# Joined decay products, joined rope products and a tile of their own for the experts' scaled outputs in a fused two-block transformer

## The chip, the cores and the metric

The program runs on one core of one Trainium2 chip. The metric is the device time of one execution in microseconds, from three executions: a median of 2303.01, with 2300.93 and 2308.81 as the ends. One further execution was profiled.

## The reference, cut to what matters

One sequence of 512 rows (16 meta rows are added for the first block) with 1024 features goes through three layers. All arithmetic is float32.

```python
# first block: differential attention + convolution, then 16 experts that each choose 66 rows
h = h + expert_choice_ffn(rms_norm(h, ffn_norm_g), w_router, w_gate, w_up, w_down)
# second block, layer 1 (mlstm): four heads; weights of the past decay by sums of log f
d = b[..., :, None] - b[..., None, :] + ib[..., None, :]
p = einsum("bhtd,bhsd->bhts", q, k) * exp(d - m_t)
# second block, layer 2 (mla): eight heads; a score has a part of 128 features and a rope part of 64
sc = einsum("bqhd,bkhd->bhqk", q, k) * QK_HEAD ** -0.5      # QK_HEAD = 128 + 64
```

Each expert computes `(silu(x @ w_gate) * (x @ w_up)) @ w_down`, scales the result by the row's gate and adds it to the rows that it chose.

## The kernel before, in words

A float32 product is made of TensorE products in a float32 format of fewer bits: an operand is split into a high part (ScalarE copy, `K.split`, L191 or L164 for weights) and a low part, the remainder (VectorE, L192 or L165), and high-high, low-high and high-low are added in PSUM (`TRIPLES`). Nearly all products go through `K.mm` (L198), so rows of the profile are told apart by their tiles. Instructions are written in the program's order by generators that are interleaved by weights, and a scheduler then sets the order on each engine; only TensorE's order in the experts is pinned (`K.pin`). On ScalarE and VectorE the order is kept once it is set: an instruction that waits holds those behind it.

**Experts** (about 370 to 1480 us). Weights come as 384 loads of 1 MB, queued on SP by `w_dma` (L138) into a ring of 17 buffers (`K.ring`). For each load two ScalarE copies (`wh`, L164) and two VectorE remainders (`wl`, L165) are made into four buffers each, so these run a few products ahead of TensorE. For each expert and each half f of its hidden features, TensorE makes G (gate), then U (up); ScalarE takes silu of G into tile `sa` (L1029), VectorE multiplies by U (L1033), TensorE transposes the product. After both halves TensorE makes Y (down). `scatter` (L992, L993) scales Y into `ys`, which is again a tile `sa`, of which there is one buffer, and GpSimd issues an indirect DMA that adds it to `acc_d` in DRAM. The next expert's silu of its first half writes the same buffer, so it waits until that DMA has read it. PSUM holds one buffer each for G, U, Y and T; G of the second half may start only when silu has read G of the first. The tiles `K.xs` (four of 128x1024) hold the residual rows before the experts; they are written out to `acc_d` ahead of the experts and loaded again from it at expert 14.

**mLSTM layer** (about 1480 to 1920 us). Gate pre-activations of the four heads are made as rows (`ig`, `fg`, 4x512), and a chain on VectorE gives `bm` and, per chunk S and later chunk T, the sums `tot`. Tile `RR` (128x512, zeroed on GpSimd) holds chunk S's rows on partitions 32S to 32S+3, and is split into `R2` (high, low). In `gen_attn`, for each head and S, the decay exponents reach all partitions by two products of four rows each (`sel[d, h]` with high and low, `S<-R,cr` in the trace, 512 - 128S columns) and a causal mask product (`S<-cr`, 128 columns). Then follow the products of q and k (`S<-q,k`) and projections of other heads (`P`).

**MLA layer** (about 1920 to 2306 us). Per pair of heads, `gen_T` transposes q and k through the PSUM tile `T` (two buffers): `qT`, `kT` for the 128 features, `qpT`, `kpT` for the rope features, where head 0 of the pair lies on partitions 0 to 63 and head 1 on 64 to 127. `gen_attn` makes, for each head and query tile t, scores of 128(t+1) columns: three products of 128 rows (`S<-kT,qT`), three of 64 rows (`S<-kpT,qpT`) and a mask (`S<-maskr`, 128 columns). `softmax_T` takes the maximum, the exponential into one of three `e` buffers, scales and transposes it (L1206, `T<-ident,e`), `K.split` fills `pT`, and after four tiles the products with v follow. Beside it run projections (`P`) of the next pairs. `rope_rows` (L1770 to L1772) makes the rope of a q pair from one GpSimd and two VectorE operations for each half, with a temporary tile `rb2` of its own.

## Time and profile before

| | us |
|---|---|
| median of three runs (lowest, highest) | 2303.01 (2300.93, 2308.81) |
| the profiled execution | 2307.86 |
| its span, first to last instruction | 2306.1 |
| TensorE busy | 2200.1 (95%) |
| VectorE busy | 1774.5 (77%) |
| ScalarE busy | 1469.8 (64%) |
| GpSimd busy | 235.5 (10%) |

The time of the profiled execution is 1.8 us longer than its span and 4.85 us (0.2%) above the median. Busy time of TensorE is the union of its matmuls, which are pipelined: the distance between two starts, not the length of one, tells what a matmul costs in a stream.

### The profile page before, as it was taken

To read this page: it belongs to the slowest core of one execution; us is meant where nothing else is said; L and a number is where in the kernel's file an instruction comes from. 1 tells how busy PE (TensorE), PEld (TensorE's weight loads), DVE (VectorE), ACT (ScalarE), POOL (GpSimd) and SP (SyncE) were. 2 spreads that over 40 slices of the span, in tenths; PEclk is the share of its full clock that TensorE was granted. 3 is DMA by queue.
4 is the path that set the end of the run, shared out by engine and by line. 5 is a ranking of instruction groups with operands and counts; after the bars stand their busy time and mean duration, and the time that the engine had idled before them with its cause. 6 is when DMAs were issued, how large, how long until landed. Compare 5 with 4: busy or idle time off the path is not lost.

```text
span 2306.1 us, 33188 instructions
## 1 busy us (share of the span) xinstructions
PE 2200.1 (95%) x12311; PEld 1647.0 (71%) x12311; DVE 1774.5 (77%) x2615; ACT 1469.8 (64%) x2193; POOL 235.5 (10%) x248
## 2 busy tenths in 40 slices
PE   7899988999999999999999999899999999899999
PEld 6899875655555555555555555688888899777779
DVE  5966577988888888888898899866665746676762
ACT  4765346777777777777777788754454624555551
POOL 2111261000000000000000011410000000010000
PEclk9999998999999999999999999999999999999999
DMA  5312778999999999999999799342322233211122
GB/s 176 88 56 67 259 276 300 378 376 359 379 369 371 371 367 365 370 372 372 374 365 364 294 376 386 130 156 76 103 90 73 83 120 114 66 49 60 51 92 74
DMA packets 204416, 528.56 MB, mean 229 GB/s; under 512 B 13362, under 2 KB 94896, under 8 KB 204254
## 3 DMA queue, kind: packets, MB, share of 16 engines
q1 hardware_dynamic: 196157, 507.64, 60.7%
q0 software_dynamic: 5488, 13.93, 2.3%
q10 hardware_dynamic: 2608, 4.87, 0.6%
q8 instruction: 97, 1.59, 0.3%
q14 instruction: 66, 0.53, 0.1%
HBM read 506.41 MB, written 17.82 MB: 227 GB/s over the span
## 4 chain that ended last, share of the span: by engine, by line
PE 79%; ACT 3%; DVE 2%; issue 1%; DMA 0%; POOL 0%; SPq 0%; ACTq 0%; DVEq 0%; POOLq 0%
PE P L198 24%; PE G L198 16%; PE Y L198 15%; PE U L198 14%; PE S L198 4%; PE O L198 3%; PE T L203 1%; DVE wl L165 1%; ACT wh L164 1%; ACT sa L1029 1%; PE T L1880 0%; PE T L1206 0%; PE T L1173 0%; PE T L1104 0%; DMA xg<-hn_d,idx 0%
## 5 line engine op out<-in xcount | busy, mean ns | idle before, releaser
L165 DVE TENSOR_TENSOR wl<-raw,wh 128x1024 fp32r<-128x1024 f32 (+1 forms) x586 | 710.0, 1224 | 150.7 <-ACT wh L164 139.5
L164 ACT ACTIVATE wh<-raw 128x1024 fp32r<-128x1024 f32 (+1 forms) x604 | 634.6, 1056 | 274.7 <-PE P L198 64.5
L198 PE MATMUL G<-wh,xgT 128*66 128x512 f32 x1024 | 280.7, 396 | 21.5 <-ACT sa L1029 20.7
L198 PE MATMUL Y<-wh,hT 128*66 128x512 f32 x1024 | 278.4, 393 | 0.0
L198 PE MATMUL U<-wh,xgT 128*66 128x512 f32 x1024 | 277.9, 393 | 0.0
L165 DVE TENSOR_TENSOR wl<-h,wh 128x1024 fp32r<-128x1024 f32 x196 | 239.5, 1237 | 26.6 <-ACT wh L164 22.8
L198 PE MATMUL P<-hT,wh 128*128 128x512 f32 x768 | 247.7, 395 | 0.0
L164 ACT ACTIVATE wh<-h 128x1024 fp32r<-128x1024 f32 x200 | 210.7, 1060 | 57.1 <-PE G L198 22.5
L198 PEld LDWEIGHTS G<-wh,xgT 128*66 128x66 f32 x1024 | 138.2, 137 | 120.1 <-ACT sa L1029 27.0
L198 PEld LDWEIGHTS U<-wh,xgT 128*66 128x66 f32 x1024 | 139.9, 137 | 97.0
L198 PEld LDWEIGHTS Y<-wh,hT 128*66 128x66 f32 x1024 | 137.4, 137 | 90.6
L198 PEld LDWEIGHTS P<-hT,wh 128*128 128x128 f32 x768 | 143.4, 188 | 29.3
L198 PE MATMUL U<-wl,xgT 128*66 128x512 f32 x512 | 159.9, 394 | 0.8 <-DVE wl L165 0.8
L198 PE MATMUL G<-wl,xgT 128*66 128x512 f32 x512 | 160.2, 394 | 0.0
L198 PE MATMUL Y<-wl,hT 128*66 128x512 f32 x512 | 159.8, 393 | 0.0
L198 PE MATMUL P<-wh,hT 128*128 128x256 f32 (+2 forms) x712 | 148.4, 291 | 5.5 <-ACT hT L191 3.2
L198 PE MATMUL P<-hT,wl 128*128 128x512 f32 x384 | 151.3, 394 | 0.0
L165 DVE TENSOR_TENSOR wl<-mx,wh 128x1024 fp32r<-128x1024 f32 x96 | 116.8, 1228 | 13.8 <-ACT wh L164 12.2
L198 PE MATMUL P<-h,wh 128*128 128x264 f32 x640 | 122.5, 286 | 1.8 <-ACT qraw L427 1.0
L198 PEld LDWEIGHTS P<-wh,hT 128*128 128x128 f32 x712 | 117.3, 191 | 7.6 <-ACT hT L191 3.9
L164 ACT ACTIVATE wh<-mx 128x1024 fp32r<-128x1024 f32 x96 | 101.3, 1061 | 27.3 <-PE Y L198 9.6
L198 PE MATMUL P<-wl,hT 128*128 128x256 f32 (+2 forms) x408 | 117.0, 289 | 0.0
(648 smaller groups left out, 3918.7 us busy)
## 6 DMA issues: line engine op xcount, KB each, us to landing
raw<-w_gate SPq DMA_DIRECT2D x82, 1024.0 KB, 7.1
raw<-w_down SPq DMA_DIRECT2D x80, 1024.0 KB, 9.1
raw<-w_up SPq DMA_DIRECT2D x76, 1024.0 KB, 7.2
h<-w_up SPq DMA_DIRECT2D x35, 1024.0 KB, 6.7
h<-w_down SPq DMA_DIRECT2D x32, 1024.0 KB, 8.9
h<-w_gate SPq DMA_DIRECT2D x31, 1024.0 KB, 6.9
raw<-a_w_in SPq DMA_DIRECT2D x24, 1024.0 KB, 5.5
mx<-w_up SPq DMA_DIRECT2D x17, 1024.0 KB, 7.2
```

Of the source, the lines that this page charges most:

```text
L164: self.nc.scalar.activation(hv, v[:, r], AF.Copy)
L165: lo.tensor_tensor(lv, v[:, r], hv.bitcast(F32), op=OP.subtract)
L198: self.last_mm = self.nc.tensor.matmul(out, l, r, start=st, stop=sp)
L203: i = self.nc.tensor.transpose(out, src, ident)
L1029: silu = nc.scalar.activation(hh, g[:CAP], AF.Silu)
```

## The change

It has three parts.

1. Experts: `ys` is no longer a tile `sa` but the first 66 rows of `K.xs[e % 2]`, two buffers that lie idle between the writing of `acc_d` and its loading.
2. mLSTM layer: the gate rows are made twice (weights and biases doubled, 8 rows instead of 4). `RR` becomes two tiles of 8 rows (from the `hn` buffers), whose columns hold the chunks one behind the other (512 + 384 + 256 + 128 = 1280). `R2` becomes one tile of 128 x 1280, zeroed on GpSimd; rows 0 to 3 hold the high parts and rows 4 to 7 the low parts: ScalarE rounds, and VectorE makes `rounded * low + r` with `low` 0 or -1. `sel` has a one in rows h and 4+h. A decay tile is then one product of 128 rows instead of two of 4.
3. MLA layer: `qpT[i]` holds head i's high parts on its own 64 partitions and its low parts on the other 64; `kpT[i][0]` holds head i's high parts on both halves and `kpT[i][1]` its low parts on both. The rope scores are then two products of 128 rows instead of three of 64 (low-low comes in besides). For this, `qpT` takes 2 ScalarE and 2 VectorE operations of 64 rows instead of 1 and 1 of 128, and `kpT` 4 and 4 instead of 1 and 1, for each of four pairs, and two tiles of 128x512 more. Room for these is made by `pT` with 10 blocks instead of 13, which for t = 2 and 3 is filled by two splits instead of one (16 ScalarE and 16 VectorE operations more in all), and by the rope's temporary, which now takes one of the three `e` buffers.

```diff
--- before.py
+++ after.py
@@ -41,9 +41,10 @@
     slot = np.broadcast_to(np.arange(1, CAP + 1, dtype=np.float32), (128, CAP))
     sel = np.zeros((128, 4), np.float32)
     for h in range(4):
-        sel[h::32, h] = 1.0
+        sel[[h, 4 + h], h] = 1.0
     ntri = np.where(p[None, :] > p[:, None], -1e30, 0.0).astype(np.float32)
-    out["c_mask"] = np.concatenate([sel, ntri], 1)
+    low = np.where((p >= 4) & (p < 8), -1.0, 0.0).astype(np.float32)[:, None]
+    out["c_mask"] = np.concatenate([sel, ntri, low], 1)
     bm = np.where((p[:, None] < 64) & (p[None, :] >= 64), -1e30, 0.0)
     out["c_bmisc"] = np.concatenate([np.broadcast_to(inv, (128, 32)), bm], 1).astype(np.float32)
     out["c_iota"] = np.arange(128, dtype=np.float32)[None, :]
@@ -988,10 +989,10 @@
 
     def scatter(y, e):
 
-        ys = K.t(p, [CAP, 2, 512], F32, "sa")
-        nc.scalar.activation(ys, y[:CAP], AF.Copy, scale=K.gate[:, e:e + 1])
+        ys = K.xs[e % 2][:CAP]
+        nc.scalar.activation(ys.rearrange("p (a b) -> p a b", a=2), y[:CAP], AF.Copy, scale=K.gate[:, e:e + 1])
         nc.gpsimd.indirect_dma_start(out=K.acc_d, out_offset=bass.IndirectOffsetOnAxis(ap=K.idx[:, e:e + 1], axis=0),
-                                     in_=ys.rearrange("p a b -> p (a b)"), in_offset=None, compute_op=OP.add)
+                                     in_=ys, in_offset=None, compute_op=OP.add)
         gather(K, e + 2)
         if e == K.ne - 2:
             for t in range(4):
...
@@ -1306,11 +1308,12 @@
 def a_pre2(K):
     nc, p, ident = K.nc, K.pools["apre"], K.ident
     w8, cs2 = K.src
-    wif = K.t(p, [128, 8, 36], F32, "wif")
+    wif = K.t(p, [128, 8, 40], F32, "wif")
     nc.gpsimd.memset(wif, 0.0)
-    nc.gpsimd.tensor_copy(wif[:, :, 0:4], w8[:, :, 0:4])
-    nc.gpsimd.tensor_copy(wif[:, :, 32:36], w8[:, :, 4:8])
-    K.wifs = [K.t(p, [128, 8, 36], F32R, f"wif{i}") for i in range(2)]
+    for i in (0, 4):
+        nc.gpsimd.tensor_copy(wif[:, :, i:i + 4], w8[:, :, 0:4])
+        nc.gpsimd.tensor_copy(wif[:, :, 32 + i:36 + i], w8[:, :, 4:8])
+    K.wifs = [K.t(p, [128, 8, 40], F32R, f"wif{i}") for i in range(2)]
     K.split(K.wifs[0], K.wifs[1], wif)
     K.cr = K.t(p, [128, 6, 128], F32R, "cr")
     nc.gpsimd.tensor_copy(K.cr[:, 0:4], cs2[:, 0:4, None].to_broadcast([128, 4, 128]))
@@ -1409,14 +1412,17 @@
     cr = K.t(p1, [128, 6, 128], F32R, "cr")
     nc.gpsimd.tensor_copy(cr, K.cr)
     sel = cr[:, 0:4]
+    offs = [0, 512, 896, 1152]
+    R2 = K.t(p1, [128, 1280], F32R, "R2")
+    nc.gpsimd.memset(R2.bitcast(F32), 0.0)
 
 
     o = K.t(ps, [128, 512], F32, "P", 3)
-    K.acc(o[:36], [(K.wifs[a][:, k], hT[b][:, k]) for k in range(8) for a, b in TRIPLES])
-    row = lambda name: K.t(p, [4, 512], F32, name)
+    K.acc(o[:40], [(K.wifs[a][:, k], hT[b][:, k]) for k in range(8) for a, b in TRIPLES])
+    row = lambda name: K.t(p, [8, 512], F32, name)
     ig, f, t1, t2, lf = row("ig"), row("fg"), row("t1"), row("t2"), row("lf")
-    nc.vector.tensor_scalar(ig, o[0:4], K.gb[:, 0:1], None, op0=OP.add)
-    nc.vector.tensor_scalar(f, o[32:36], K.gb[:, 1:2], None, op0=OP.add)
+    nc.vector.tensor_scalar(ig, o[0:8], K.gb[:, 0:1], None, op0=OP.add)
+    nc.vector.tensor_scalar(f, o[32:40], K.gb[:, 1:2], None, op0=OP.add)
     nc.vector.tensor_scalar_mul(t1, f, -1.0)
     nc.vector.tensor_tensor(t1, t1, f, op=OP.min)
     nc.scalar.activation(t1, t1, AF.Exp)
@@ -1432,7 +1438,7 @@
     bm = row("t1")
     nc.vector.tensor_sub(bm, b, m)
     nc.vector.tensor_sub(ig, ig, b)
-    tot = K.t(p, [4, 4, 4], F32, "tot")
+    tot = K.t(p, [8, 4, 4], F32, "tot")
     for S in range(4):
         for T in range(S + 1, 4):
             e = b[:, 128 * T - 1:128 * T]
@@ -1440,21 +1446,23 @@
                 nc.vector.tensor_copy(tot[:, S, T:T + 1], e)
             else:
                 nc.vector.tensor_add(tot[:, S, T:T + 1], tot[:, S, T - 1:T], e)
-    RR = K.t(p, [128, 512], F32, "RR")
-    nc.gpsimd.memset(RR, 0.0)
+
+    RR = [K.t(p, [128, D], F32, "hn", 2)[:8] for _ in range(2)]
     for S in range(4):
-        d = slice(32 * S, 32 * S + 4)
-        nc.vector.tensor_copy(RR[d, 128 * S:128 * S + 128], bm[:, 128 * S:128 * S + 128])
+        r, of = RR[S // 2], offs[S] - offs[S // 2 * 2]
+        nc.vector.tensor_copy(r[:, of:of + 128], bm[:, 128 * S:128 * S + 128])
         for T in range(S + 1, 4):
-            ts = slice(128 * T, 128 * T + 128)
-            nc.vector.tensor_scalar(RR[d, ts], bm[:, ts], tot[:, S, T:T + 1], None, op0=OP.add)
-    R2 = [K.t(p1, [128, 512], F32R, f"R{i}") for i in range(2)]
-    K.split(R2[0], R2[1], RR)
+            at = of + 128 * (T - S)
+            nc.vector.tensor_scalar(r[:, at:at + 128], bm[:, 128 * T:128 * T + 128], tot[:, S, T:T + 1], None, op0=OP.add)
+    for r, (a_, b_) in zip(RR, ((0, 896), (896, 1280))):
+        rt = R2[:8, a_:b_]
+        nc.scalar.activation(rt, r[:, :b_ - a_], AF.Copy)
+        nc.vector.scalar_tensor_tensor(rt, rt.bitcast(F32), K.src[1][:8, 132:133], r[:, :b_ - a_], op0=OP.mult, op1=OP.add)
     o = K.t(ps, [128, 512], F32, "T", 2)
     for t in range(4):
         ts = slice(128 * t, 128 * t + 128)
-        nc.tensor.transpose(o[:, 8 * t:8 * t + 4], ig[:, ts], ident[:4, :4])
-        nc.tensor.transpose(o[:, 8 * t + 4:8 * t + 8], m[:, ts], ident[:4, :4])
+        nc.tensor.transpose(o[:, 8 * t:8 * t + 4], ig[:4, ts], ident[:4, :4])
+        nc.tensor.transpose(o[:, 8 * t + 4:8 * t + 8], m[:4, ts], ident[:4, :4])
     cb = K.t(p1, [128, 4, 8], F32, "cb")
     nc.vector.tensor_copy(cb, o[:, :32].rearrange("p (t x) -> p t x", x=8))
     em = K.t(p1, [128, 4, 4], F32, "em")
@@ -1465,7 +1473,6 @@
     p = pa_.enter_context(tc.tile_pool(name="a2", bufs=1, reuse_waits="tile"))
     K.p_pq = tc.tile_pool(name="aq", bufs=1, side="right", reuse_waits="tile")
     pq = K.p_pq.__enter__()
-    offs = [0, 512, 896, 1152]
     qkv = {("v", 0): v0}
 
     def gen_v(h):
@@ -1515,10 +1522,8 @@
         for S in range(4):
             n = 512 - 128 * S
             ss = slice(128 * S, 128 * S + 128)
-            d = slice(32 * S, 32 * S + 4)
             bc = K.t(ps, [128, 512], F32, "S", 2)
-            K.mm(bc[:, :n], sel[d, h], R2[0][d, 128 * S:], True, False)
-            K.mm(bc[:, :n], sel[d, h], R2[1][d, 128 * S:], False, False)
+            K.mm(bc[:, :n], sel[:, h], R2[:, offs[S]:offs[S] + n], True, False)
             K.mm(bc[:, :128], cr[:, 4], cr[:, 5], False, True)
             wt = K.t(p, [128, 512], F32, "e", 3)
             nc.scalar.activation(wt[:, :n], bc[:, :n], AF.Exp, bias=cb[:, S, h:h + 1])
@@ -1766,7 +1771,8 @@
         x1, x2 = src[:, :, :, 0:32], src[:, :, :, 32:64]
         d1, d2 = dst[:, :, :, 0:32], dst[:, :, :, 32:64]
         for d, a, b, op in ((d1, cos, sin, OP.subtract), (d2, sin, cos, OP.add)):
-            tb = K.t(pool, sh, F32, f"rb{heads}")
+            tb = K.t(pool, sh, F32, "rb1") if heads == 1 else \
+                K.t(pool, [128, 512], F32, "e", 3)[:, :256].rearrange("p (t h d) -> p t h d", t=4, h=2)
             nc.gpsimd.tensor_tensor(d, x1, a, op=OP.mult)
             nc.vector.tensor_mul(tb, x2, b)
             nc.vector.tensor_tensor(d, d, tb, op=op)
@@ -1870,6 +1876,9 @@
         qkv["kv", pr] = ks, kp, v
         yield 0
 
+    BASE = (0, 3, 5, 6)
+    HALVES = [(slice(0, 64), slice(64, 128)), (slice(64, 128), slice(0, 64))]
+
     def gen_T(pr):
         qs, qp, rq = qkv["q", pr]
         ks, kp, v = qkv["kv", pr]
@@ -1878,8 +1887,25 @@
             o = K.t(ps, [128, 4, 128], F32, "T", 2)
             for t in range(4):
                 nc.tensor.transpose(o[:, t], src(t), ident)
+            o = o.rearrange("p t s -> p (t s)")
+            if name == "qpT":
+
+                d = [K.t(pq, [128, 512], F32R, f"{name}{i}") for i in range(2)]
+                for i, (r, x) in enumerate(HALVES):
+                    nc.scalar.activation(d[i][r], o[r], AF.Copy)
+                    nc.vector.tensor_sub(d[i][x], o[r], d[i][r].bitcast(F32))
+                return d
+            if name == "kpT":
+
+                d = [[K.t(pq, [128, 512], F32R, f"{name}{i}{b}") for b in range(2)] for i in range(2)]
+                for i, (r, x) in enumerate(HALVES):
+                    for y in (r, x):
+                        nc.scalar.activation(d[i][0][y], o[r], AF.Copy)
+                    for y in (r, x):
+                        nc.vector.tensor_sub(d[i][1][y], o[r], d[i][0][r].bitcast(F32))
+                return d
             d = [K.t(pq, [128, 512], F32R, f"{name}{i}") for i in range(2)]
-            K.split(d[0], d[1], o.rearrange("p t s -> p (t s)"), gain)
+            K.split(d[0], d[1], o, gain)
             return d
 
         qT = [tr(lambda t: qs[:, t, hh, 0:128], f"qT{hh}", None) for hh in range(2)]
@@ -1893,24 +1919,26 @@
         qT, kT, qpT, kpT, v, rq = qkv[pr]
         for hh in range(2):
 
-            pT = [K.t(p, [128, 13, 128], F32R, f"pT{i}") for i in range(2)]
-            hs = slice(64 * hh, 64 * hh + 64)
+            pT = [K.t(p, [128, 10, 128], F32R, f"pT{i}") for i in range(2)]
             for t in range(4):
                 n = 128 * (t + 1)
                 ts = slice(128 * t, n)
                 s = K.t(ps, [128, 512], F32, "S", 2)
                 terms = [(qT[hh][a][:, ts], kT[hh][b][:, :n]) for a, b in TRIPLES]
-                terms += [(qpT[a][hs, ts], kpT[b][hs, :n]) for a, b in TRIPLES]
+                terms += [(qpT[hh][:, ts], kpT[hh][b][:, :n]) for b in range(2)]
                 for i, (l, r_) in enumerate(terms):
                     K.mm(s[:, :n], l, r_, i == 0, False)
                 K.mm(s[:, ts], maskr[:, 1], maskr[:, 0], False, True)
                 pt = softmax_T(K, p, ps, s[:, :n], rq[:, t, hh:hh + 1], t + 1)
-                K.split(*(x[:, t:t + 3 * t + 1:3] for x in pT), pt)
+                n = min(t + 1, 2)
+                K.split(*(x[:, t:t + 3 * n - 2:3] for x in pT), pt[:, :n])
+                if t > 1:
+                    K.split(*(x[:, 5 + t:2 * t + 4] for x in pT), pt[:, 2:])
                 yield 600 + 400 * t
             o = K.t(ps, [128, 512], F32, "O", 1)
             for c in range(4):
                 for i, (a, b) in enumerate(TRIPLES):
-                    K.mm(o[:, 128 * c:], v[a][:, c, hh], pT[b][:, 4 * c:3 * c + 4],
+                    K.mm(o[:, 128 * c:], v[a][:, c, hh], pT[b][:, BASE[c] + c:BASE[c] + 4],
                          c == 0 and i == 0, c == 3 and i == 2)
             mx = mixed(2 * pr + hh)
             nc.vector.scalar_tensor_tensor(mx, o, 0.5, mx, op0=OP.mult, op1=OP.mult)
```

The scheduler orders the changed program anew. Up to the first expert's scaling the order of ScalarE is unchanged. Three places:

ScalarE in the experts, from the scaling of one expert's Y (`sa<-Y,gate` before, `x<-Y,gate` now) over the weights' high parts to the silu of the next expert's first half (`sa<-G`). Before:

```order
L992 ACTIVATE sa<-Y,gate 66x1024
L164 ACTIVATE wh<-raw 128x1024 x12
L164 ACTIVATE wh<-h_6853 128x1024 x2
L164 ACTIVATE wh<-h_6877 128x1024 x2
L1029 ACTIVATE sa<-G 66x1024
L164 ACTIVATE wh<-h_6899 128x1024 x2
L191 ACTIVATE hT_7082<-T 128x528
```

and in the changed program:

```order
L993 ACTIVATE x_2787<-Y,gate 66x1024
L165 ACTIVATE wh<-raw 128x1024 x8
L1030 ACTIVATE sa<-G 66x1024
L165 ACTIVATE wh<-raw 128x1024 x4
L165 ACTIVATE wh<-h_6849 128x1024 x2
L165 ACTIVATE wh<-h_6873 128x1024 x2
L165 ACTIVATE wh<-h_6895 128x1024 x2
L192 ACTIVATE hT_7077<-T 128x528
```

The silu stood behind 16 copies of weights and stands behind 8. Of the 15 experts that follow a scaling, 13 had 16 copies there and two had 11; in the changed program all have 8.

TensorE in the MLA layer, the last score tile (512 columns) of the first pair's second head. Before:

```order
L198 MATMUL S<-kT_18858,qT_18831 128x512
L198 MATMUL S<-kT_18858,qT_18832 128x512
L198 MATMUL S<-kT_18859,qT_18831 128x512
L198 MATMUL S<-kpT_18867,qpT_18840 128x512
L198 MATMUL S<-kpT_18867,qpT_18841 128x512
L198 MATMUL S<-kpT_18868,qpT_18840 128x512
L198 MATMUL S<-maskr 128x128
L198 MATMUL O<-pT_18908,v 128x512 x2
```

and in the changed program:

```order
L199 MATMUL P<-hT_17972,wh 128x512
L199 MATMUL S<-kT_18835,qT_18806 128x512
L199 MATMUL S<-kT_18835,qT_18807 128x512
L199 MATMUL S<-kT_18836,qT_18806 128x512
L199 MATMUL S<-kpT_18846,qpT_18816 128x512
L199 MATMUL S<-kpT_18847,qpT_18816 128x512
L1207 MATMUL T<-ident,e 128x128 x2
L199 MATMUL S<-maskr 128x128
L199 MATMUL P<-hT_17972,wl 128x512
```

Two rope products stand where three stood, and this tile moved behind projections (`P`); before it followed on the head's other score tiles.

TensorE in the mLSTM layer, the second decay tile (384 columns) of the second head. Before:

```order
L198 MATMUL P<-hT_13780,wh 128x512
L198 MATMUL P<-hT_13780,wl 128x512
L198 MATMUL S<-R_14206,cr 128x384
L198 MATMUL S<-R_14207,cr 128x384
L198 MATMUL S<-cr 128x128
L198 MATMUL P<-hT_13781,wh 128x512
L198 MATMUL S<-q_14948,k_14828 128x512
```

and in the changed program:

```order
L199 MATMUL P<-hT_13770,wh 128x512
L199 MATMUL P<-hT_13769,wh 128x512
L199 MATMUL P<-hT_13769,wl 128x512
L199 MATMUL S<-R_14128,cr 128x384
L199 MATMUL S<-cr 128x128
L199 MATMUL P<-hT_13770,wh 128x512
L199 MATMUL P<-hT_13769,wh 128x512
L199 MATMUL S<-q_14935,k_14815 128x512
```

One product stands where two stood; the neighbours are of the same kinds.

## Rows read from the trace of the kernel before

**Rows 1.** Windows: length, busy PE, PEld, DVE, ACT, POOL; clock, DMA share, GB/s.

```profile
370.00:1480.00 1110.00, 1088.31 (x5005) 653.09 (x5003) 994.32 (x873) 878.96 (x871) 74.45 (x51) 1.00 0.97 360
1480.00:2000.00 520.00, 499.76 (x3047) 442.75 (x3047) 338.93 (x765) 252.65 (x533) 44.01 (x51) 0.98 0.32 99
2000.00:2307.00 307.00, 291.25 (x1790) 251.71 (x1789) 189.39 (x502) 148.43 (x424) 18.52 (x13) 0.97 0.20 63
```

**Rows 2.** Waits of PE: total us, times, longest.

```profile
PE G L198 <- ACT sa L1029: 20.7, 13, 1.6
```

**Rows 3.** Timeline, one expert's start: start us, us, engine, line, operation [idle before].

```profile
707.98 1.50 POOL L993 DMA_INDIRECT acc_d<-sa,idx  x1 [8.02 <-ACT sa L992]
...
728.72 1.00 ACT L1029 ACTIVATE sa<-G 66x1024 f32<-66x1024 f32 x1
...
729.77 1.14 PE L198 MATMUL G<-wh,xgT 128*66 128x512 f32 x4 [1.59 <-ACT sa L1029]
```

**Rows 4.** Tile sa: its DMAs (the scatters).

```profile
DMA to landing us min/median/max: 8.1/8.6/9.4
```

**Rows 5.** Windows in the experts, without and with G's waits.

```profile
430.00:500.00 70.00, 70.00 (x323) 42.06 (x322) 62.99 (x55) 56.74 (x57) 4.67 (x3) 1.00 1.01 380
500.00:570.00 70.00, 68.41 (x315) 40.92 (x314) 62.51 (x54) 55.17 (x55) 3.72 (x3) 1.00 1.00 368
```

**Rows 6.** Waits of SP's queue, the longest.

```profile
SPq L138 <- DVE wl L165: 1235.0, 401, 19.2
```

**Rows 7.** Timeline of PE, two score tiles of the MLA layer.

```profile
2070.94 0.68 PE L198 MATMUL S<-kT,qT 128*128 128x384 f32 x3
...
2072.43 0.91 PE L198 MATMUL S<-kT,qT 128*128 128x512 f32 x3
2073.28 0.97 PE L198 MATMUL S<-kpT,qpT 64*128 64x512 f32 x3
2074.18 0.33 PE L198 MATMUL S<-maskr 128*128 128x128 f32 x1
2074.34 0.51 PE L1206 MATMUL T<-ident,e 128*128 128x128 f32 x3
2074.61 0.42 PE L198 MATMUL P<-wh,qlT 128*128 128x384 f32 x1
```

**Rows 8.** Timeline of PE, products of 128 rows and 384 columns in a stream.

```profile
1573.99 1.23 PE L198 MATMUL S<-q,k 128*128 128x384 f32 x6
1575.06 0.39 PE L198 MATMUL P<-hT,wh 128*128 128x512 f32 x1
```

**Rows 9.** Timeline of PE, a decay tile of 384 columns (mLSTM layer).

```profile
1633.68 0.39 PE L198 MATMUL P<-hT,wl 128*128 128x512 f32 x1
1634.00 0.60 PE L198 MATMUL S<-R,cr 4*128 4x384 f32 x2
...
1634.99 0.39 PE L198 MATMUL S<-q,k 128*128 128x512 f32 x1
```

**Rows 10.** Tile kpT and line 446: durations min/median/max ns, first and last start.

```profile
L191 ACT ACTIVATE kpT<-T x4: 597/599/604, 2012.6 to 2176.2; 128x512 fp32r<-128x512 f32 x4
L192 DVE TENSOR_TENSOR kpT<-T,kpT x4: 681/681/693, 2013.3 to 2177.0; 128x512 fp32r<-128x512 f32 x4
...
L446 ACT ACTIVATE kh<-t x16: 631/644/647, 64.5 to 112.1; 64x528 fp32r<-64x528 f32 x16
```

**Rows 11.** Tile R: its split and the first product that reads it.

```profile
L198 PE MATMUL S<-R,cr x32: 268/356/500, 1546.1 to 1810.5; 4*128 4x512 f32 x8, 4*128 4x384 f32 x8, 4*128 4x256 f32 x8, 4*128 4x128 f32 x8
...
L192 DVE TENSOR_TENSOR R<-RR,R x1: 675/675/675, 1544.0 to 1544.0; 128x512 fp32r<-128x512 f32 x1
```

**Rows 12.** Window of the first pair's second head.

```profile
2024.90:2035.10 10.20, 10.20 (x35) 8.06 (x35) 5.92 (x19) 4.42 (x12) 0.00 (x0) 0.50 0.00 0
```

**Rows 13.** Tile qp: the rope's GpSimd and VectorE operations.

```profile
L1770 POOL TENSOR_TENSOR qp<-qs,trig x8: 716/861/1331, 1991.9 to 2151.7; 128x256 f32<-128x256 f32 x8
L1772 DVE TENSOR_TENSOR qp<-qp,rb x8: 407/411/426, 1994.6 to 2156.7; 128x256 f32<-128x256 f32 x8
```

More of the change, by code (lines that the diff above doesn't have):

```diff
@@ L1292, in a_pre @@
     nc.gpsimd.dma_start(K.gbc[:, 1], A["a_norm_2"].to_broadcast([128, D]))
-    K.gb = K.t(p, [4, 2], F32, "gb")
-    nc.gpsimd.dma_start(K.gb[:, 0:1], A["a_ig_bias_2"].rearrange("a h -> h a"))
-    nc.gpsimd.dma_start(K.gb[:, 1:2], A["a_fg_bias_2"].rearrange("a h -> h a"))
-    w8, cs2 = K.src = K.t(p, [128, 8, 8], F32, "w8"), K.t(p, [128, 132], F32, "cs2")
+    K.gb = K.t(p, [8, 2], F32, "gb")
+    for i in (0, 4):
+        nc.gpsimd.dma_start(K.gb[i:i + 4, 0:1], A["a_ig_bias_2"].rearrange("a h -> h a"))
+        nc.gpsimd.dma_start(K.gb[i:i + 4, 1:2], A["a_fg_bias_2"].rearrange("a h -> h a"))
+    w8, cs2 = K.src = K.t(p, [128, 8, 8], F32, "w8"), K.t(p, [128, 133], F32, "cs2")
     nc.gpsimd.dma_start(w8, A["a_w_in_2"][0].rearrange("(c p) n -> p c n", p=128)[:, :, 5120:5128])
@@ L1308, in a_pre2 @@
     w8, cs2 = K.src
-    wif = K.t(p, [128, 8, 36], F32, "wif")
+    wif = K.t(p, [128, 8, 40], F32, "wif")
     nc.gpsimd.memset(wif, 0.0)
-    nc.gpsimd.tensor_copy(wif[:, :, 0:4], w8[:, :, 0:4])
-    nc.gpsimd.tensor_copy(wif[:, :, 32:36], w8[:, :, 4:8])
-    K.wifs = [K.t(p, [128, 8, 36], F32R, f"wif{i}") for i in range(2)]
+    for i in (0, 4):
+        nc.gpsimd.tensor_copy(wif[:, :, i:i + 4], w8[:, :, 0:4])
+        nc.gpsimd.tensor_copy(wif[:, :, 32 + i:36 + i], w8[:, :, 4:8])
+    K.wifs = [K.t(p, [128, 8, 40], F32R, f"wif{i}") for i in range(2)]
     K.split(K.wifs[0], K.wifs[1], wif)
```

## The prediction

> **What bounds the kernel.** I read busy time by stage first. The windows [rows 1] show TensorE busy for 1088 of 1110 us in the experts, 500 of 520 in the mLSTM layer with the start of the next, and 291 of the last 307. It bounds every stage, so the change can act in two ways only: take away idle time of TensorE, or make its stream shorter. The list of waits names the idle time: 20.7 us in 13 waits for `sa` in the experts [rows 2]; nearly all that the 1110 us lose (21.7). For the stream I read timelines of TensorE and take distances between starts [rows 7 to 9].
>
> **Experts.** In the timeline of one expert [rows 3] the scatter is issued at 707.98 us; the DMAs of `sa` land after 8.6 us at the median [rows 4], so at about 716.6 the tile is free. The silu that writes it next starts only at 728.72, and G's products of the second half 1.05 us later, after 1.59 us of waiting. So it is not the DMA itself that is late: the silu stands late in ScalarE's order. It has 16 weight copies ahead of it since the scaling of Y, and 8 in the changed program (the order above). ScalarE's mean instruction in the experts is 879/871 = 1.01 us [rows 1], so eight fewer in front put it up to 8 us earlier, against 1.59 that are missing. The two experts with 11 copies account for 15 less 13 waits. I take the whole 20.7 us away. The new tile adds no instruction; its two buffers lie idle in this stretch, and a buffer comes back after two experts, 2 x 1110/16 = 139 us. Silu earlier puts the copies behind it 1.0 us later, once per expert; they run ahead of TensorE by their four buffers, and I cost them at nothing. Without that cover it would be 15 x 1.0 = 15 us, and part 1 would keep 6.
>
> What is late next is the weights. The loads are queued by SP, which waits 1235 us in 401 waits for a free ring buffer [rows 6], so the queue is ahead, not behind. A stretch without waits has TensorE at 70.00 of 70 us with 380 GB/s, one with a wait 368 [rows 5]: more was moved when more was wanted. The DMA share is 1.00 in both, however, so I keep a rival.
>
> **mLSTM layer.** The decay tile of 384 columns [rows 9]: five products (a projection, high, low, mask, a projection) between 1633.68 and 1634.99, 1.31 us. A 128-row product of 384 columns in a stream costs (1575.06 - 1573.99)/6 = .178 [rows 8], so one of 512 about .238 (an estimate by columns); one of 128 columns (2074.61 - 2074.34)/3 = .09 [rows 7]. Changed, there are two of 512, one of 384 and a mask, all of 128 rows: .238 + .178 + .09 + .238 = .744, which saves .57. Of this .178 is the product that falls away, the other .39 the passage from 128 rows to 4 and back, which the row shows as time that neither side's products explain. By the same .39 the tiles of 512, 256 and 128 columns save .63, .51 and .48: 2.19 for a head, **8.8 us** for four. If the passage costs nothing more than the row by chance, it is only the products that fall away (.238 + .178 + .119 + .09 = .63 a head), 2.5 us.
>
> Ahead of this, `R2` is made by two pairs of operations on 8 rows of 896 and 384 columns instead of a pair on 128 x 512 (675 ns, ending at 1544.7; the first decay product starts at 1546.1 [rows 11]). 1280 columns for 512 take about 1.7 us per engine in place of .675, two engines one after the other: up to 2 us later, of which 1.4 is free. Projections stand around it on TensorE; I cost it at nothing, at most .7 if they are used up. The doubled bias loads, weight copies on GpSimd and the larger memset run long before they are read, and GpSimd is busy 44 of 520 us [rows 1].
>
> **MLA layer.** The tile of 384 columns: from 2070.94 to 2072.43, 1.49 us for seven products [rows 7]. Changed: five of 384 and a mask, 5 x .178 + .09 = .98; saves .51. For 512 columns: 2072.43 to 2074.34, 1.91, against 5 x .238 + .09 = 1.28; saves .63. Of .51, .178 is the third rope product and .33 the passage to 64 rows and back; by the same .33, 256 and 128 columns save .45 and .42. Sum 2.01 for a head, **16.1 us** for eight. The lower end, the products alone, is 8 x .63 = 5.0.
>
> The three 64-row products of 512 columns take 2074.18 - 2073.28 = .90 us [rows 7], where three in a stream would take .71: they run one after the other. The Trainium skill (TensorE: Matmul & The Clock Gate, Part 3: Packing small matmuls — row/col tiling) says that products of fewer than 128 rows in different row groups overlap in the array, which speaks against filling the rows. Here the three of a head share one group of rows and one PSUM tile, and the trace shows no overlap; what the rule would make of the sum is a rival below.
>
> The price: for `qpT` and `kpT` two operations per engine and pair become six. Half the partitions don't make them cheaper: a 64-row copy of 528 columns takes 644 ns, a 128-row one of 512 takes 599 [rows 10]. Four more per engine and pair, four pairs: 16 x .60 on ScalarE, 16 x .68 on VectorE, 10.9 us, and 32 small splits of `pT` besides. ScalarE is busy 148 and VectorE 189 of 307 us [rows 1], so the throughput hides there; without that cover the whole 10.9 and about 5 for the splits would show. What is not hidden by throughput is the PSUM tile T under `kpT`: it was held .60 + .68 = 1.3 us and will be held 4 x (.60 + .68) = 5.1, and there are only two. Upper bound: 3.8 us for each of four pairs, 15 us; lower bound 0, as the projections (the moved tile of the order above stands among them) let TensorE go on. I take 1 us per pair, **4 us**, nearer to 0 because only transposes wait for T, and by the code they come in a few bursts per pair.
>
> A stretch of 10.2 us ran at a granted clock of 0.50 [rows 12], the lower of the two levels, 1.2 GHz. It lies in the first pair, whose order changes; it may go (-5 us) or come anew (+5). I take 0 and keep 5 for the range.
>
> **Sum.** -20.7 - 8.8 - 16.1 + 4 = -41.6 against the profiled execution's 2307.9 gives 2266.3. That execution lies 4.85 us above the median of the runs; from the median, 2261.
>
> **Rivals.**
> 1. *The weights become the bound of the experts.* For: DMA share 1.00, and 0.97 over the stage [rows 1, 5]. Against: SP's waits for buffers [rows 6], 380 GB/s when asked [rows 5]. If the loads can't come faster than they did, part 1 gives nothing: 2303 - 8.8 - 16.1 + 4 = 2282. The Trainium skill (DMA: Bandwidth & Descriptors, Where 436 GB/s comes from) says that transfers from HBM are bound by about 358 GB/s for a core, which is this rival; another page of it (Perfetto Trace Analysis, Roofline) lets a lone core go to about 435. The 380 measured agrees with the second.
> 2. *The last block's gain is eaten by its new waits.* For: T held four times as long, three `e` buffers shared by four users, 64 more operations on engines whose order TensorE follows; the upper bound of T's wait alone, 15, is nearly the 16.1. Against: the idle halves of ScalarE and VectorE. Parts 1 and 2 remain: 2303 - 20.7 - 8.8 = 2274.
> 3. *The 64-row products already overlap.* Then the three cost as two, the change saves nothing there and still pays 4: 2303 - 20.7 - 8.8 + 4 = 2278. Against: the .90 us above.
> 4. *Slower: the `e` ring.* A rope's temporary takes an `e` buffer while it waits for the next pair's projections, and the softmax behind it on ScalarE waits with it; TensorE then waits for the softmax's transposes. It decides from 49 us on (41.6 and the 7 that a measurement needs), 16 for each of three pairs that are followed by another. The rope itself holds two buffers for .86 + 2 x .41 = 1.7 us each, 3.4 a pair [rows 13]; only if projections lie between would it come to 16. Then about 2310.
>
> **How the numbers follow.** The forecast, 2261, has .62. Its own range, 2254 to 2272: above by 15 instead of 4 in T's wait (+11), below by the half clock gone (-5) and a free T (-2 of the 4). Rival 1 has .10 (2282), rival 2 .20 (2274), rival 3 .02 (2278), rival 4 .02 (2310); .04 is for better than 2254. The range reaches over rivals 1 to 3 and a little below: 2251 to 2284. About 0.3% (6.9 us) is what a measurement of this kernel can tell from no change. Only rival 4 ends slower, .02. Within 0.3% is where rival 2's waits, or those with rival 1, eat nearly all, .03 of rival 2's .20. Faster is the rest: .62 + .10 + .17 + .02 + .04 = .95.
>
> **What would show it.** Right: no wait of G for `sa`, the experts about 20 us shorter at some 370 GB/s; decay tiles with one 128-row product and no gap, 384 columns in about .74 us with their two projections; score tiles of .98 and 1.28 us; TensorE's waits for `T` or `kpT` in the last block grown by 4 us. Wrong: G or U waiting for `wh`, `wl` or loads in the experts; tile distances of 1.31, 1.49 and 1.91 as before; waits of T's transposes for `e`, or of `S` for `kpT`, of 15 us or more.

## The result and the profile after

The changed kernel takes 2293.26 us at the median of 7 runs (2291.53 to 2295.74), the kernel before 2303.03 in the same comparison; the ratio is 0.9937, its interval [0.9923, 0.9951]. That is 9.8 us faster by the medians and 14.5 by the ratio, where 42 were forecast; 2293 is outside the range given (2251 to 2284). The kernel before came out near 2301 us in some executions and near 2309 in others, so that its median moves between 2303 and 2312 from one comparison to the next, and the ratios carry that. The profiled execution took 2293.82 us with a span of 2292.0.

The windows of the changed kernel, first the three of [rows 1], then the first of [rows 5], at the end two short ones in the mLSTM layer (columns as there):

```profile
370.00:1480.00 1110.00, 1100.91 (x5074) 661.17 (x5072) 974.59 (x882) 849.71 (x879) 78.98 (x60) 1.00 0.97 360
1480.00:2000.00 520.00, 497.98 (x3036) 446.96 (x3036) 339.13 (x776) 252.21 (x542) 38.40 (x47) 0.97 0.32 99
2000.00:2307.00 307.00, 267.11 (x1680) 238.02 (x1680) 194.71 (x514) 155.21 (x441) 15.70 (x12) 0.97 0.19 63
430.00:500.00 70.00, 70.00 (x323) 42.06 (x322) 62.97 (x55) 56.70 (x57) 4.64 (x3) 1.00 1.01 383
...
1569.00:1575.00 6.00, 4.93 (x26) 4.69 (x27) 5.05 (x12) 3.51 (x10) 0.45 (x1) 0.72 0.53 158
1652.00:1660.00 8.00, 5.90 (x26) 5.80 (x27) 5.60 (x22) 4.36 (x16) 0.00 (x0) 0.57 0.01 2
```

TensorE's waits for weights and operands in the experts, of the changed kernel; `sa` [rows 2] is no longer among them:

```profile
PE U L199 <- DVE wl L166: 2.9, 2, 1.7
PE Y L199 <- ACT wh L165: 2.1, 1, 2.1
PE Y L199 <- DVE wl L166: 1.7, 10, 0.2
PE G L199 <- DVE wl L166: 0.8, 5, 0.2
...
PE U L199 <- ACT wh L165: 0.7, 1, 0.7
```

The timeline of TensorE, a decay tile (beside [rows 9]) and two score tiles (beside [rows 7]):

```profile
1623.55 0.40 PE L199 MATMUL P<-hT,wl 128*128 128x512 f32 x1
1623.78 0.34 PE L199 MATMUL S<-R,cr 128*128 128x384 f32 x1
1623.96 0.22 PE L199 MATMUL S<-cr 128*128 128x128 f32 x1
1624.02 0.68 PE L199 MATMUL P<-hT,wh 128*128 128x512 f32 x2
...
2134.89 0.69 PE L199 MATMUL S<-kT,qT 128*128 128x384 f32 x3
2135.43 0.51 PE L199 MATMUL S<-kpT,qpT 128*128 128x384 f32 x2
2135.77 0.22 PE L199 MATMUL S<-maskr 128*128 128x128 f32 x1
...
2139.02 0.95 PE L199 MATMUL S<-kT,qT 128*128 128x512 f32 x3
2139.80 0.62 PE L199 MATMUL S<-kpT,qpT 128*128 128x512 f32 x2
2140.26 0.22 PE L199 MATMUL S<-maskr 128*128 128x128 f32 x1
```

Tile by tile the joined products do what was worked out. A tile of 384 columns spans .88 us up to its mask product, one of 512 columns 1.24; with .06 us for the mask (1624.02 - 1623.96) that is .94 and 1.30, forecast .98 and 1.28. The decay tile with its two projections takes .23 + .18 + .06 + .26 (half of the .51 for two) = .73, forecast .74, before 1.31.

So the question is where the gain went. I cut both profiles at the same products (first G, last Y, first key projection of the memory rows, first output projection, first transpose of the MLA layer, last mask of a score, end) and split each stage in three: *idle*, no matmul runs; *lower clock*, busy time x (1 - granted clock) summed over windows of 1 us, an estimate of what the lower level costs; *stream*, the rest. Before and after, us:

| stage | length | idle | lower clock | stream |
|---|---|---|---|---|
| up to the experts | 359.2, 359.2 | 49.3, 47.7 | 8.6, 11.4 | 301.3, 300.1 |
| experts | 1114.6, 1105.6 | 21.5, 8.7 | 1.7, 3.5 | 1091.5, 1093.5 |
| memory rows | 20.9, 20.2 | 5.9, 5.5 | 0.0, 0.0 | 14.9, 14.7 |
| mLSTM layer | 355.1, 353.4 | 3.3, 5.6 | 2.3, 6.7 | 349.5, 341.0 |
| to the MLA layer | 122.0, 123.3 | 3.5, 3.7 | 1.7, 3.0 | 116.8, 116.6 |
| MLA layer | 245.0, 237.9 | 14.9, 24.4 | 10.2, 7.4 | 219.9, 206.1 |
| end | 86.0, 89.2 | 4.4, 4.9 | 1.4, 4.5 | 80.2, 79.8 |

The stream of the two attention layers fell by 8.5 and 13.8 us (forecast 8.8 and 16.1), but idle time and the lower clock took 6.7 of it in the one and 6.7 in the other. The experts gave 9.0 instead of 20.7. The change in all, -14.0, is that of two profiled executions; 4.3 of it comes in because the profiled execution of before lies 4.8 above its median and that of after .6.

The longest new wait of the mLSTM layer, TensorE and then VectorE; first before, then the changed kernel:

```profile
1664.10 0.47 PE L198 MATMUL P<-wh,hT 128*128 128x256 f32 x2 [1.47 <-DVE rst L222]
...
1654.10 0.80 PE L199 MATMUL P<-wh,hT 128*128 128x256 f32 x2 [3.21 <-DVE m_q L1121]
```

```profile
1650.93 0.16 DVE L1545 TENSOR_SCALAR st<-O 128x1 f32<-128x1 f32 x1 [3.37 <-PE O L199]
...
1653.62 0.42 DVE L1121 COPY m_q<-P 128x256 f32<-128x256 f32 x1
```

In both kernels the copy of `m_q`, which frees a tile P, starts 2.7 us after the first operation on a head's result `O` (1653.62 and 1650.93; before 1663.52 and 1660.83). Before, TensorE had projections left after the products `O` until 1662.63; in the changed order those stand ahead of `O`, and nothing covers the chain.

### The profile page after: what moved, and what is told of

Same layout as the page of the kernel before. It is cut to its first block, busy times and chain, and to the rows that moved or that the text cites. A ratio compares the mean times of both kernels' runs of the same rounds, so it can differ in the third digit from the quotient of the medians.

```text
span 2292.0 us, 33030 instructions
## 1 busy us (share of the span) xinstructions
PE 2188.3 (95%) x12263; PEld 1647.5 (72%) x12263; DVE 1761.3 (77%) x2648; ACT 1446.8 (63%) x2226; POOL 232.2 (10%) x252
## 4 chain that ended last, share of the span: by engine, by line
PE 76%; DVE 4%; ACT 2%; issue 2%; DMA 0%; DVEq 0%; ACTq 0%
PE P L199 24%; PE Y L199 15%; PE U L199 15%; PE G L199 14%; PE O L199 4%; PE S L199 2%; DVE wl L166 2%; PE T L204 1%; ACT wh L165 0%; PE T L1889 0%; PE T L1174 0%; PE T L1207 0%; PE T L1105 0%; DMA xg<-hn_d,idx 0%; DVE kpT L1905 0%
## 5 line engine op out<-in xcount | busy, mean ns | idle before, releaser
L166 DVE TENSOR_TENSOR wl<-raw,wh 128x1024 fp32r<-128x1024 f32 (+1 forms) x586 | 695.6, 1227 | 137.1 <-ACT wh L165 133.4
L165 ACT ACTIVATE wh<-raw 128x1024 fp32r<-128x1024 f32 (+1 forms) x604 | 612.6, 1049 | 198.6 <-PE P L199 69.1
L166 DVE TENSOR_TENSOR wl<-h,wh 128x1024 fp32r<-128x1024 f32 x196 | 233.5, 1237 | 24.0 <-ACT wh L165 22.7
L165 ACT ACTIVATE wh<-h 128x1024 fp32r<-128x1024 f32 x200 | 202.8, 1053 | 26.7 <-PE U L199 9.7
L199 PEld LDWEIGHTS Y<-wl,hT 128*66 128x66 f32 x512 | 69.1, 137 | 53.1 <-DVE wl L166 7.2
```

The costliest lines, as they stand in the source:

```text
L165: self.nc.scalar.activation(hv, v[:, r], AF.Copy)
L166: lo.tensor_tensor(lv, v[:, r], hv.bitcast(F32), op=OP.subtract)
L199: self.last_mm = self.nc.tensor.matmul(out, l, r, start=st, stop=sp)
```

## Experiments

Edited kernels are compared with one another by their medians, and by the stages of one profiled execution each.

**Each part alone, and without the third.** The edits are hunks of the diff:

```diff
p1: +        ys = K.xs[e % 2][:CAP]
p2: +            K.mm(bc[:, :n], sel[:, h], R2[:, offs[S]:offs[S] + n], True, False)
p3: +                terms += [(qpT[hh][:, ts], kpT[hh][b][:, :n]) for b in range(2)]
```

> The kernel before with part 1 alone (the experts' own tiles for the scaled outputs). Theory A, each part loses in its own place: the wait for sa goes, but the new order of ScalarE runs one weight load less ahead from some expert on and the last expert loses to late weights; the first product after the experts starts about 9 us earlier, total 2294 (-9). Theory B, the parts are worth what was forecast and it is their joint order that loses: -20.7, 2282. Theory C, the weight loads are the bound: no change, 2303.

> The kernel before with part 2 alone (joined decay products). Theory A: TensorE's stream in the mLSTM layer is about 8.5 us shorter as forecast, but new waits and stretches at the lower clock give most of it back: 2301 (-2). Theory B: -8.8, 2294.

> The kernel before with part 3 alone (joined rope products). Theory A: the stream of the MLA layer is about 14 us shorter, waits for kpT, kT and the softmax of the first pair grow by about 10 us: 2299 (-4). Theory B: -12, 2291.

> Parts 1 and 2 without the rope products. Theory A: the sum of the two, about -11: 2292, so that the rope products are worth nothing on top of it (the whole change measured 2293.3). Theory B: -29.5, 2273.5.

Measured: 2298.44 us (ratio 0.9969 [0.9955, 0.9982]), 2302.79 (0.9993 [0.9979, 1.0006]), 2302.31 (0.9986 [0.9972, 0.9999]) and 2301.13 (0.9973 [0.9956, 0.9989]). By the ratios that is 7.1, 1.6, 3.2 and 6.2 us. Theory A is the nearer one for the parts alone (with part 1 alone the first product after the experts comes 9.0 us earlier, as it has it): no part is worth its forecast even alone (the interval of part 2 includes no change), and the three add up to 11.9 of the whole change's 14.5, so no interplay is needed for the loss. For parts 1 and 2 together theory A failed: 2292 was expected, and 2301.13 is 7.9 above the whole change, so part 3 is worth something on top of the others (7.1 us in its own layer, 245.0 against 237.9, 2.8 of it lower clock). By stages: part 1 alone takes the experts to 1106.0 us; part 2 alone has a stream of 340.7 in its layer, with idle 5.6 and lower clock 6.0; part 3 alone has a stream of 205.8 in the MLA layer with idle 24.4. These are nearly the numbers of the whole change.

**The experts: order or loads?** In the changed kernel an expert takes 67.9 us from the second to the sixth, then 68.6 to 68.7, and the last one 78.5 where it took 72.3 before. I counted how long a high part is ready before TensorE first uses it: at least 2.76 us from the second expert to the fifteenth before the change; in the changed kernel as much up to the fifth, .99 in the sixth, .50 from then on. In ScalarE's order that is one place: in the sixth expert 10 copies stand between the second silu and the next split where 12 stand elsewhere, and from there on the copies are one load later against everything else. TensorE then waits for the remainder, as in this piece of its timeline and of VectorE's:

```profile
884.91 0.68 PE L199 MATMUL Y<-wl,hT 128*66 128x512 f32 x2 [0.16 <-DVE wl L166]
```

```profile
882.50 1.22 DVE L1034 TENSOR_TENSOR sa<-sa,U 66x1024 f32<-66x1024 f32 x1 [1.06 <-PE U L199]
883.64 1.21 DVE L166 TENSOR_TENSOR wl<-mx,wh 128x1024 fp32r<-128x1024 f32 x1
```

The .16 shown is the idle part; the distance between starts grows by .3 to .4, twice per expert. The first test, e5, writes the order out, with the copies a load earlier:

```diff
+                if self.pin2:
+                    self.tc.keep_in_program_order(c_)
...
+        if K.n_get < K.n_exp - 8 and K.n_cv < K.n_get + 2:
+            K.w_cv()
```

> The changed kernel, with the copies of a weight load issued one load earlier in the experts and the order of ScalarE and VectorE there written out (weight copies, silu, product, scalings and splits in program order), so that the copies of high parts stay one load further ahead of TensorE from the sixth expert on, as they are up to there. Theory A (the order's lead is what was lost from the sixth expert on): the two short waits for wl per expert go, an expert takes 67.9 us throughout instead of 68.6 to 68.8, about 6.5 us in all: 2287 against 2293. Rival (the weight loads arrive no faster, the lead is only where it shows): experts stay at 68.7 and wait elsewhere, for wh or loads: 2293.

Measured 2290.71 us (0.9907 [0.989, 0.9923]). Half a miss: the ready time stayed at 2.77 and the waits for `wl` went in all experts but the last, but my order had the product of silu and U behind one remainder more, and TensorE waited for it (68.5 us per expert):

```profile
PE T L212 <- DVE sa L1050: 4.5, 14, 0.3
```

The next kernel, e9, has it where the changed kernel's first experts have it, between the two remainders of a load:

```diff
+            if self.mid is not None:
+                self.mid()
+                self.mid = None
             parts[0].append(hv)
```

> As the kernel with the written order, but with the product of silu and U on VectorE between the two remainders of one load, where the changed kernel has it in its first experts (behind both, TensorE waited for that product 14 times in the run before this one). Theory A (the order's lead alone makes the difference): every expert from the second to the fifteenth takes 67.9 us, no wait for wl or sa above 0.1 us up to the last expert, its first product after the experts 6 us earlier than in the changed kernel: 2287. Rival (weight loads bound the stretch): 68.5 us again, with the wait on another tile: 2291.

Measured 2278.27 us (0.9884 [0.9855, 0.9913]), 15 below the changed kernel by the medians, 12 by the ratios, and the fastest of all. Every expert from the second to the fifteenth takes 67.9 us. A window in the experts:

```profile
800.00:1300.00 500.00, 500.00 (x2298) 300.63 (x2297) 453.65 (x392) 402.04 (x398) 33.69 (x24) 1.00 0.99 371
```

TensorE is busy for all of 500 us with the DMA share still at .99: the weights are not the bound, rival 1 is out. Of the 15 us, 9.3 lie in the experts (1105.6 to 1096.3, more than the 6 expected: 6.9 in the nine experts, 2.6 in the last, where Y no longer waits for `wh`). The rest is mostly the lower clock in stages that this edit does not touch, 3.8 less in the mLSTM layer and 3.1 at the end.

**The last expert.** Beside these 6.9 us (nine experts, .72 to .82 each) the changed kernel loses 6.1 there against the kernel before. U waits for `wl` (2.9, before .8) and Y for `wh` (2.1, before not at all). VectorE and GpSimd in the changed kernel:

```profile
1426.34 2.36 DVE L166 TENSOR_TENSOR wl<-h,wh 128x1024 fp32r<-128x1024 f32 x2
1429.65 5.74 DVE L166 TENSOR_TENSOR wl<-h,wh 128x1024 fp32r<-128x1024 f32 x2 [0.96 <-ACT wh L165]
```

```profile
1427.71 6.59 POOL L853 TENSOR_TENSOR mt<-mt,gm 128x1024 f32<-128x1024 f32 x2 [27.84 <-ACT mt L852]
```

Two remainders take 5.74 us beside GpSimd's multiplications of the memory rows, 2.36 alone; they end 1.09 us after GpSimd does (1435.39 and 1434.30), about the length of one remainder alone. The Trainium skill (SBUF — State Buffer, SBUF: two separate sides) says that GpSimd and a VectorE instruction with two SBUF inputs lock a port pair against each other: the one that starts first has it for the whole instruction. The trace agrees, by these ends.

```diff
-    K.nc.gpsimd.tensor_tensor(mt, mt, gain, op=OP.mult)
+    (eng or K.nc.gpsimd).tensor_tensor(mt, mt, gain, op=OP.mult)
```

> The changed kernel, with the two multiplications of the memory rows by their gain (128x1024, in the last expert) on VectorE instead of GpSimd. Theory A (VectorE's remainders take 2.9 instead of 1.2 us beside GpSimd, and that makes TensorE wait for wl in the last expert): the two waits of U for wl there, 2.9 us in all, go; VectorE has 2 x 1.2 us more to do: 2291 against 2293. Rival (the last expert's weights are late through the order alone): the waits stay, 2293 to 2295.

> The changed kernel with the written order of the run e9 and the memory rows on VectorE. Theory A, both gains: 2284 to 2285. Rivals of both: 2293.

Measured 2287.27 us (0.9921 [0.9892, 0.995]) and 2280.43 (0.9893 [0.9864, 0.9923]). VectorE now takes 2.35 for each pair:

```profile
1428.77 2.35 DVE L853 TENSOR_TENSOR mt<-mt,gm 128x1024 f32<-128x1024 f32 x2
1431.04 2.35 DVE L166 TENSOR_TENSOR wl<-h,wh 128x1024 fp32r<-128x1024 f32 x2
```

U's wait for `wl` is 1.2 us instead of 2.9, and the experts are 2.6 us shorter than in the changed kernel (1.4 of it lower clock), 3.0 shorter with the written order (1093.3; 21.3 less than before the change). So what part 1 promised is there once order and last expert are mended. The time of the second kernel did not follow, since its mLSTM layer and end had 6.2 us more of the lower clock than the run with the written order alone.

**The MLA layer: which wait?** Three edits aim at the longer hold of T and the late `kpT`: the rope rows of k laid out twice before the transposes (e6: one operation per engine and head instead of two, and the first head's transposes ahead of those of k), their transposes ahead of those of k (e7), and their transposes in a tile P (e11). A fourth kernel, e8, has the edits of e5 and e6.

```diff
e6: -        kpT = tr(lambda t: kp[:, t].rearrange("p h d -> p (h d)"), "kpT", None)
e6: +            return tr(lambda t: x[:, t].rearrange("p c d -> p (c d)"), f"kpT{hh}", None)
e11: +            o = K.t(ps, [128, 4, 128], F32, *(("P", 3) if name == "kpT" else ("T", 2)))
```

> The changed kernel, with the rope rows of k laid out twice side by side for each head before the transposes, so that a PSUM tile T comes out with head i's k on both halves and is split by one ScalarE and one VectorE operation of 128 rows, instead of eight operations of 64 rows on one tile. Adds 4 transposes and one GpSimd product for each pair. Theory A (the time for which T and kpT are held is what the MLA layer waits for): TensorE's idle time there, 24 us, falls by about 5 to 7: 2287. Rival (the waits come from the shorter stream itself, which reaches the same chain of softmax and splits sooner): idle time stays at 22 to 25 us, the four transposes cost 1.5 us: 2294.

> The changed kernel, with the transposes of the rope rows of k ahead of those of k's 128 features, so that their long split runs while kT is made. Theory A (kpT is late because it is last): the waits of S for kpT, 3 to 4 us in all, go and those for kT take a part of it over: 2291. Rival: kT's wait grows by as much, 2293.

> The changed kernel with both edits, the written order in the experts and the rope rows of k laid out twice. They act in different stages, so both theories of gain together give 2281; with the rivals of both 2294.

> The changed kernel, with the transposes of the rope rows of k in a PSUM tile of the projections (P, three buffers) instead of T (two). Theory A (T held for about 5 us is what the next transposes wait for): idle time of TensorE in the MLA layer falls from 24 to about 20 us, waits of P grow by less: 2290. Rival (S waits for kpT itself, not the next transposes for T): idle time as before, 24 us, or more by waits for P: 2293 to 2297.

Measured 2293.72 us (0.9926 [0.991, 0.9943]), 2302.57 (0.9965 [0.9953, 0.9977]), 2291.91 (0.9912 [0.9895, 0.9928]) and 2294.47 (0.9952 [0.9936, 0.9968]). Idle time in the layer: 21.6, 29.3, 21.7 and 29.5 us, against 24.4. None is a way out: with fewer operations the idle time fell by 2.8, less than the 5 to 7 expected, and the lower clock took 5.7 more; e8, which was to give 2281, shows the same. The transposes first made the layer longer (250.3 us against 237.9), the other tile a little (240.2), with one new wait of 7.2 us for GpSimd's rope rows. That takes T's hold under `kpT` out as the one cause: with `kpT` out of T its waits are gone, but that for `kT` stays (2.9 us) and that for `v` on VectorE grows (2.8 instead of 1.2); less the new wait the idle time is 22.3.

The next two kernels part the added operations from the shorter stream.

```diff
e14: +                terms += [(qpT[hh][:, ts], kpT[hh][b][:, :n]) for b in (0, 1, 1, 1)]
e16: +                terms += [(qpT[hh][r, ts], kpT[hh][b][r, :n]) for r, b in ((own, 0), (own, 1), (own, 1))]
```

> The changed kernel with two more rope products of 128 rows in each score tile (the low part of k is added two more times, which changes the result in its low digits only), 2 x 8 x .6 = 9.6 us more of stream. Theory A (operations): idle time in the MLA layer stays near 24 us, 2293 + 9.6 = 2303. Rival (shorter stream): the added products fill waits, idle time falls to about 16 us and the time stays at 2293 to 2296.

> The changed kernel with all its new tiles and splits in the MLA layer, but the rope scores from three products of 64 rows of a head's own half: high-high and two times low part of k (low-high is left out, high-low stands twice, which changes the result in its low digits only). The operations are the changed kernel's, TensorE's stream is the old one. Theory A (the added operations on ScalarE and VectorE make TensorE wait, whatever its stream): idle time in the MLA layer stays at 22 to 28 us with a stream of 220 us: 2293 + 14 = 2307. Rival (the shorter stream only reaches the same chains sooner): idle time falls back to about 15 us, 2298.

Measured 2302.99 us (0.9986 [0.9971, 1.0001]) and 2308.20 (1.0013 [0.9998, 1.0027]). The longer stream (216.1) did not fill the waits, idle time was 27.9. With the old kind of products it was 20.3, between the two theories, the total at that of the first: by these two executions about 5.4 of the 9.5 us come with the operations and 4.1 are there only with joined products. The split is rough, since this stream (224.1) is 4.2 longer than the old one. Some waits of TensorE in the MLA layer, before the change,

```profile
PE T L1880 <- DVE qT L192: 1.7, 2, 1.0
...
PE S L198 <- ACT kpT L191: 0.9, 2, 0.5
...
PE S L198 <- ACT kT L194: 0.2, 1, 0.2
```

of the changed kernel

```profile
PE S L199 <- ACT kT L195: 3.6, 4, 1.4
...
PE T L1889 <- DVE qT L193: 2.7, 3, 1.0
...
PE S L199 <- DVE kpT L1905: 1.7, 2, 0.9
PE T L1207 <- DVE e L1204: 1.6, 3, 0.8
...
PE S L199 <- ACT kpT L1903: 1.2, 1, 1.2
PE S L199 <- ACT e L1202: 1.2, 3, 0.7
```

and of the one with 64-row products:

```profile
PE S L199 <- ACT kT L195: 3.6, 4, 1.4
...
PE T L1889 <- DVE qT L193: 2.4, 3, 1.0
...
PE S L199 <- DVE kpT L1905: 0.5, 1, 0.5
...
PE T L1207 <- DVE e L1204: 0.3, 1, 0.3
...
PE S L199 <- ACT kpT L1903: 0.3, 1, 0.3
```

The wait for `kT` comes with the operations, whatever the products; those for `kpT` and the softmax's `e` shrink with the longer 64-row products. For the longest of the waits for `kT`, in the second pair, the changed kernel's trace shows how:

```profile
2052.39 0.59 ACT L1895 ACTIVATE qpT<-T 64x512 fp32r<-64x512 f32 x1 [1.00 <-DVE qpT L1896]
2053.01 0.69 ACT L195 ACTIVATE kT<-T,gcol 128x512 fp32r<-128x512 f32 x1
...
2053.74 0.74 PE L199 MATMUL S<-kT,qT 128*128 128x128 f32 x4 [1.39 <-ACT kT L195]
```

The copy of `kT` stands on ScalarE behind the second 64-row copy of `qpT`, which the change added and which waits 1.0 us for VectorE. In the other pairs the copy of `kT` does not stand behind a wait of that kind, and what moved it there stays open. So does why 9.6 us more of 128-row products left 27.9: every edit orders the engines anew.

Last, the price of part 3 with the experts mended:

> The run e9 (written order in the experts) without part 3, the old rope products and splits. It prices part 3 beside the mended experts: by the stages of the runs before, -14 us of stream, +9.5 us of idle time and the lower clock as it falls, 3 to 7 us slower than e9, 2281 to 2285. If part 3 is worth nothing beside other waits: 2278.

Measured 2290.14 us (0.9939 [0.9916, 0.9962]), 11.9 above the run with the written order and part 3, where 3 to 7 were expected: a miss. In the MLA layer itself 7.6 (244.8 against 237.2: stream 219.9 and 206.2, idle 14.6 and 24.4, lower clock 10.2 and 6.7); 3.3 and 3.0 more are the lower clock in the mLSTM layer and at the end. Part 3 pays, by 3.9 us of stream less idle time, of 12.1 forecast. The lower clock in its layer can't be counted for it: with the old products that was 10.2 us in this run and before, but 5.1 with part 1 alone and 3.4 with part 2 alone.

## Why the prediction was wrong, point by point

Between the two profiled executions 41.6 us were forecast and 14.0 came. Of the 27.6 that are missing, 11.7 are the experts, 5.5 the idle time in the MLA layer above the 4 that were priced, 2.3 the idle time in the mLSTM layer, 2.6 the stream of both layers, and 8.8 the lower clock outside the experts; 3.3 went the other way in the other stages.

- **The wait for `sa`.** Right: it was the order, and it went. Wrong is the step "Silu earlier puts the copies behind it 1.0 us later ... I cost them at nothing": I had compared the orders from scaling to silu and left the rest of the expert alone, where one load of lead is lost in the sixth. The price without that cover was bounded (15 us, "part 1 would keep 6"); 9.0 were kept, but that these are near is luck: the loss is not 1.0 us in each of 15 experts, it is 6.9 in nine together and 6.1 in the last. "What is late next is the weights" named the wrong thing: not the loads, but the remainders made from them, and in the last expert VectorE beside GpSimd, for which the prediction has no term.
- **Decay products.** The term of 8.8 measured 8.5; the passage to 4-row products was as large as the row said. The step that failed is the sum, which took stream for time. Idle time rose by 2.3: TensorE waits 3.2 us at the copy of `m_q` on VectorE where it waited 1.5 before, and .89 and .46 in the first head for the exponentials of the decay tiles; one wait of .76 went. The chain to `m_q` did not get shorter, and fewer projections of TensorE cover it.
- **`R2`.** Right: the second remainder ends at 1534.8, the first decay product starts at 1536.3 without a wait.
- **Rope products.** 16.1 measured 13.8, though the two tiles shown came out as forecast; where the 2.3 stayed is open. The wait of 4 us ("1 us per pair") measured 9.5 in all, 3.2 more in the first pair alone: it is the mis-sized term, within its bounds of 0 and 15. Its reason, T held longer under `kpT`, is not the one cause: taking `kpT` out of T, or halving its operations, left 21.6 us of idle time or more. The added 64-row operations, as long as 128-row ones (592 and 688 ns by the trace), also stand in front of `kT`'s split, which is shown for 1.4 us.
- **The clock.** "I take 0 and keep 5 for the range": the stretch in the first pair went (5.1 us of the lower clock), as it did with part 1 or part 2 alone, but others came, and all stages together have 36.5 us instead of 25.9. This was a term of its own, not an edge of the range. What decides it is not shown.
- **Rivals.** Rival 2 is the nearest to what happened, though its price (2274) left parts 1 and 2 whole. Rivals 1, 3 and 4 did not occur: the loads kept up with a TensorE that never paused (e9), the stream fell where three products became two, and waits for `e` came to 2.8 us, not 49. All but one of my cases kept at least one part whole, and that made the range too narrow.

## What to carry to other kernels

Where one engine is busy 95% of the time, taking work from it uncovers the chains behind it: price the next wait at each end of a stretch, not only the stream. When a scheduler orders a changed program anew, compare the order over the whole loop, by how far the producers stand ahead of their user in each turn, for a lead that is lost once can stay lost (here from the seventh expert to the fifteenth). And a small edit that writes the good order out can be worth about as much as the change: 9.3 us in the experts here, where the change as a whole gave 9.8.

## What the runs showed of the hardware that was not expected

Short idle times of TensorE go with a lower clock, but not each time. In the changed kernel two idle times of .9 and .5 us (to 1569.6 and to 1570.5) fall into 6 us with a granted clock of .72, and one of 3.2 us (to 1654.1) into 8 us with .57: the lower of the two levels in part of them. In the run with the written order the same three waits (.90, .46 and 3.21) left the clock at full:

```profile
1560.00:1566.00 6.00, 4.64 (x35) 4.08 (x36) 5.52 (x14) 4.62 (x11) 0.45 (x1) 1.00 0.35 94
1642.00:1651.00 9.00, 6.22 (x41) 5.64 (x42) 7.62 (x27) 5.46 (x20) 0.00 (x0) 1.00 0.01 3
```

In the stage up to the experts, where ScalarE's order is the same in the kernel before and the changed one, the lower clock cost between 8.6 and 13.8 us over all runs. Differences of 3 or 4 us between two profiled executions can be that alone. It is not only chance of one execution, though: over the whole program the granted clock was .977 to .980 in all seven runs of the changed kernel and .982 to .984 in all four of the kernel with the written order (e9). Why is open.
